# Where the gates times b2 are added in a mixture-of-experts layer: at the 7th, 13th, 19th and 25th expert in place of four experts in a row

## The chip, the cores and the metric

One core of a Trainium2 chip runs the whole kernel. The metric is the device time of one execution in microseconds (us); the kernel before took 1820.64 us, the median of 3 runs (1817.49 to 1822.31).

## The reference

The reference is one layer of a diffusion backbone over 512 latent tokens and 256 context tokens, each of width 1024: a token mixer (an RWKV-7 scan beside a Fourier mix), then a mixture of experts. Only the experts matter here:

```python
logits = h @ w_router + b_router            # h: (512, 1024), 32 experts
top_val, top_idx = lax.top_k(logits, 4)
gates = softmax(top_val)
# for each token t and each of its four experts e:
u   = h[t] @ w1[e] + b1[e]                  # 2048 wide, glu and lin interleaved
act = glu * sigmoid(1.702 * glu) * (lin + 1)   # glu, lin clamped at 7
out[t] += gate[t, e] * (act @ w2[e] + b2[e])
x = layer_norm(alpha * x + gt2 * out)
```

The term `gate * b2` needs no expert's product: over all tokens it is one matrix product, the gates (512 x 32) times b2 (32 x 1024). The kernel computes it in four parts of 128 tokens each. The change is about when these four parts run.

## The kernel before, in words

**The stage.** The expert stage starts at about 700 us of the span and ends at about 1784 us. Experts are sorted by how many tokens chose them; `PLAN` gives the order in which they run and how many rows ("cap") each may have: 128, 32, 160, 32, 96, 64, 96, 192, 32, 64, 96, 64, 160, 32, 96, 64, 96, 192, and so on. In this text e0, e1, ... are the experts in that order, so e7 and e17 are the two of 192 rows. A cap is cut in blocks of 64 rows and a last one of 32 where it isn't a multiple (`blocks`).

**One expert.** `fetch` makes one-hot matrices and indices (TensorE L1249, VectorE L1261 to L1270), casts a selector on GpSimd (L1300, three buffers), and gathers the rows from DRAM by indirect DMAs that GpSimd issues (L1305). `split` transposes them (L1316, L1318). `up` multiplies by w1 in 8 slices, `down` by w2 in 4 slices (L1337); each slice is a tile `raw` of 1 MB that SyncE loads (L1328). `turn` transposes the activations between them (L1389, L1391). `put` adds the rows to `accd` in DRAM by one accumulating indirect DMA per block (L1414), issued by GpSimd; each waits until the one before has landed, as all write the same tensor.

**The ring of weights.** The `raw` tiles have 14 buffers (`RAWA` + `RAWB`). A load is issued as soon as the multiplication that last used its buffer is through; loads run up to 14 slices ahead of TensorE. 384 such loads make the stage's traffic, one after another on SyncE's queue.

**The order.** `all_experts` is a generator of steps, run one by one by `Run`. For its `i`-th expert it yields: the fetch of the expert two ahead, the 8 slices of `up`, then `turn` of the expert before, `split` of the next, the 4 slices of `down` and the `put` of the expert before, and, for four values of `i`, one `b2_part`. Within an engine the final order is that of the planner that builds the program: it simulates the engines and may move a ready instruction ahead of one that it thinks still waits.

**One part of b2.** `b2_part(j)` takes the tile `yb` (128 x 1024, one buffer), and for each half multiplies the gates of 128 tokens by b2 (L1479) into a PSUM tile `pt`, which ScalarE copies into `yb` (L1480). Then GpSimd issues an accumulating indirect DMA of `yb` into `accd` (L1481). The tiles `pt` come from a pool of two buffers that `fetch`, `split` and `turn` use too. b2 was multiplied by gt2 earlier.

Of the kernel before, what the change touches and what calls it, by code (L numbers as in the profile page):

```python
# [1187 lines left out]
def moe(tc, I, ck, h2d, accd, modd, P):  # L1188
# [277 lines left out]
    def place(i):  # L1466
        j, cap = PLAN[i]
        return Expert(cap, rm[:, :, j], R6[:, :, j], sel3[:, j:j + 1])

    def chosen(i):  # L1470
        j = PLAN[i][0]
        return SY.value_load(eidi[0:1, j:j + 1], min_val=0, max_val=NE - 1)

    def b2_part(j):

        y = B.tile([128, D], F32, "yb", 1)
        for n in range(2):
            p = pst.tile([128, 512], F32, name="pt", tag="pt")
            PE.matmul(p, gwT[:, j * 128:(j + 1) * 128], b2r[:, n * 512:(n + 1) * 512], start=True, stop=True)  # L1479
            A.activation(y[:, n * 512:(n + 1) * 512], p, AF.Copy)  # L1480
        G.indirect_dma_start(out=accd[:, :], out_offset=bass.IndirectOffsetOnAxis(ap=toki[:, j:j + 1], axis=0),  # L1481
                             in_=y, in_offset=None, compute_op=ALU.add)

    def all_experts():
        cur, prev = first, None
        ahead = [place(i) for i in range(1, len(PLAN))]
        yield cur.split
        yield ahead[0].fetch
        for i in range(len(PLAN)):
            nxt = ahead[i] if i + 1 < len(PLAN) else None  # L1490
            if i + 2 < len(PLAN):
                yield ahead[i + 1].fetch
            ups = list(cur.up())
            yield from ups[:8 if nxt else 4]
            if nxt:
                nxt.weights(chosen(i + 1))
            if prev:
                yield prev.turn
            if nxt:
                yield nxt.split  # L1500
            if prev:
                yield from prev.down()
                yield prev.put
                if 4 <= i < 8:
                    yield lambda j=i - 4: b2_part(j)
            if not nxt:
                yield from ups[4:]
            prev, cur = cur, nxt
        yield prev.turn
        yield from prev.down()  # L1510
        yield prev.put
# [14 lines left out]
    B = Buffers(None, 99, (praw, RAWA))  # L1526
    first = Expert(PLAN[0][1], rm0, R60, M["sel0"][0:96]).weights(0)
    experts = Run(all_experts())
    experts.load(RAWA)
    sb_ = ExitStack()  # L1530
# [317 lines left out]
```

## Time and profile before

| what | value |
|---|---|
| median of 3 runs | 1820.64 us |
| the profiled execution: its own time | 1815.8 us |
| its span, first to last instruction | 1813.8 us |
| TensorE busy, share of span | 1612.2 us, 89% |
| VectorE, ScalarE, GpSimd busy | 755.1, 392.6, 431.3 us |
| mean DMA rate over the span | 316 GB/s |
| mean granted TensorE clock | 0.929 |

The profiled execution is one run; the numbers of the trace belong to it and not to the median. "Busy" of TensorE is no measure of speed, as its matmuls are pipelined and their ends modelled. In a row of the trace's answers, PE is TensorE, DVE VectorE, ACT ScalarE, POOL GpSimd and SP SyncE; `out<-in` are the program's tile names, and a name in angle brackets behind "idle before" says who ended the wait.

### The profile page before, as it was taken

What the parts mean: (1) busy time and instruction counts of PE and PEld (TensorE: products, weight loads), DVE (VectorE), ACT (ScalarE), POOL (GpSimd) and SP (SyncE); (2) the same over time, 40 slices, a digit from 0 to 9 for tenths busy, and PEclk for the clock granted to TensorE, in tenths of its full rate; (3) what the DMA queues carried; (4) which work ended last, traced back from release to release, by engine and by line L of the source; (5) the groups of instructions that cost most, each with busy time, mean ns of one, the idle gap of its engine ahead of it and who ended that gap; (6) DMA issues with size and microseconds to landing.
All of it is one profiled execution on the core that took longest, in us unless ns stands there. A gap on an engine that the chain in (4) does not pass through costs nothing. (4 is left out here: it accounts for less than half of the span.)

```text
span 1813.8 us, 38967 instructions
## 1 busy us (share of the span) xinstructions
PE 1612.2 (89%) x16148; PEld 875.3 (48%) x16148; DVE 755.1 (42%) x1775; ACT 392.6 (22%) x771; POOL 431.3 (24%) x436
## 2 busy tenths in 40 slices
PE   4889887677999977999959999999999999989982
PEld 1767655566787863454413453443244344324430
DVE  4899977887446674222111121231112211211113
ACT  3565465232223250110010000100000100001002
POOL 1444434264134341101020211111111100112112
PEclk9899888786899977999979999999999999999995
DMA  8567859675575538999996999999899999999995
GB/s 320 168 198 255 252 175 282 182 219 151 174 245 184 201 125 317 414 381 405 416 315 203 386 405 408 412 414 416 340 398 401 411 414 419 408 412 400 402 406 197
DMA packets 205508, 572.72 MB, mean 316 GB/s; under 512 B 28449, under 2 KB 116129, under 8 KB 156177
## 3 DMA queue, kind: packets, MB, share of 16 engines
q1 hardware_dynamic: 144624, 520.11, 73.9%
q0 software_dynamic: 11840, 24.91, 5.9%
q10 hardware_dynamic: 48864, 25.17, 4.8%
q8 instruction: 129, 2.11, 0.5%
q14 instruction: 51, 0.41, 0.1%
HBM read 512.57 MB, written 57.56 MB: 314 GB/s over the span
## 5 line engine op out<-in xcount | busy, mean ns | idle before, releaser
L1337 PE MATMUL st<-raw,xt 128*32 128x512 f32 (+1 forms) x6784 | 634.7, 525 | 18.9 <-DMA raw<-in_w 13.0
L1337 PEld LDWEIGHTS st<-raw,xt 128*32 128x32 f32 x6784 | 244.3, 110 | 368.8 <-issue 285.1
L1337 PE MATMUL st<-raw,at 128*32 128x512 f32 (+1 forms) x3392 | 319.3, 521 | 6.9 <-ACT at L1391 3.1
L1371 DVE TENSOR_SCALAR sg<-st 128x256 f32<-128x256 f32 x87 | 36.4, 419 | 511.5 <-PE st L1344 511.5
L1337 PEld LDWEIGHTS st<-raw,at 128*32 128x32 f32 x3392 | 111.0, 111 | 187.9 <-issue 148.6
L1372 ACT ACTIVATE sth<-sg 128x256 f32<-128x256 f32 x87 | 36.1, 415 | 719.4 <-DVE sg L1371 693.5
L1414 POOL DMA_INDIRECT accd<-y,idx x53 | 86.3, 1628 | 292.6 <-DVE y L1408 145.3
L1408 DVE SCALAR_TENSOR_TENSOR y<-st,gt,gt2h 128x512 f32<-128x512 f32 (+1 forms) x53 | 34.7, 655 | 249.0 <-PE st L1337 215.7
L1305 POOL DMA_INDIRECT xg<-h2d,idx x53 | 53.2, 1004 | 247.7 <-DVE idx L1270 228.4
L1300 POOL CAST sel<-sel 96x64 bf16<-96x64 f32 x31 | 9.2, 298 | 395.3 <-PE st L1344 376.4
L328 PE MATMUL pj<-hhi,wh 128*128 128x512 f32 (+1 forms) x240 | 90.0, 377 | 9.8 <-DVE hlo L281 9.8
L328 PE MATMUL pj<-hhi,wl 128*128 128x512 f32 (+1 forms) x240 | 90.9, 380 | 8.8 <-DVE wl L324 8.8
L328 PE MATMUL pj<-hlo,wh 128*128 128x512 f32 (+1 forms) x240 | 90.9, 379 | 0.0
L652 PE MATMUL big<-Rb,Lt 128*128 128x256 f32 (+1 forms) x192 | 51.9, 420 | 13.4 <-DVE pk L658 5.0
L1391 ACT ACTIVATE at<-pt 128x512 f32<-128x512 f32 (+1 forms) x53 | 26.8, 518 | 143.3 <-PE pt L1389 143.0
L328 PEld LDWEIGHTS pj<-hhi,wl 128*128 128x128 f32 x240 | 47.7, 199 | 20.2 <-DVE wl L324 11.0
L328 PEld LDWEIGHTS pj<-hhi,wh 128*128 128x128 f32 x240 | 47.4, 197 | 19.6 <-DVE hlo L281 10.1
L752 POOL TENSOR_TENSOR SW<-S,Wc 64x128 f32<-64x128 f32 (+1 forms) x66 | 31.3, 475 | 96.4 <-DVE S L787 76.8
L328 PEld LDWEIGHTS pj<-hlo,wh 128*128 128x128 f32 x240 | 47.5, 198 | 13.8 <-issue 7.2
L407 DVE SCALAR_TENSOR_TENSOR acc<-war,sil,acc 128x512 f32<-128x512 f32 x56 | 52.8, 943 | 0.8 <-ACT acc L404 0.6
L1318 ACT ACTIVATE xt<-pt 128x512 f32<-128x512 f32 (+1 forms) x53 | 27.0, 518 | 99.2 <-PE pt L1316 98.7
L652 PEld LDWEIGHTS big<-Rb,Lt 128*128 128x128 f32 x192 | 37.0, 230 | 20.8 <-issue 10.2
(390 smaller groups left out, 2249.3 us busy)
## 6 DMA issues: line engine op xcount, KB each, us to landing
raw<-in_w SPq DMA_DIRECT2D x384, 1024.0 KB
war<-in_w_ada SPq DMA_DIRECT2D x64, 256.0 KB
chd<-pk ACTq DMA_DIRECT2D x52, 256.0 KB
wr<-in_w_in ACTq DMA_DIRECT2D x40, 256.0 KB
wa<-in_w_ada SPq DMA_DIRECT2D x16, 512.0 KB
win<-chd SPq DMA_DIRECT2D x8, 896.0 KB
win<-chd SPq DMA_DIRECT2D x16, 448.0 KB
ltd<-Lt SPq DMA_DIRECT2D x8, 768.0 KB
```

The costliest lines, as they stand in the source:

```text
L328: PE.matmul(p, a[:, k, :], b[:, k0 + k, t0:t0 + n], start=(k0 + k == 0 and i == 0), stop=(k0 + k == KD - 1 and i == 2))
L407: V.scalar_tensor_tensor(acc, wr, sil0[:, k:k + 1], acc, op0=ALU.mult, op1=ALU.add)
L652: PE.matmul(ps[:, z], Lu[:, u0 + (z0 + z if d == 0 else 3 - z0 - z), :], Rb[:, z0 + z], start=True, stop=True)
L752: G.tensor_tensor(SW[HALF[p]].rearrange("p z d c -> p (z d) c"), S[HALF[p], :, :, p].rearrange("p z d c -> p (z d) c"), Wc[HALF[p], 2 * c0 ...
L1305: G.indirect_dma_start(out=x, out_offset=None, in_=h2h[n], in_offset=bass.IndirectOffsetOnAxis(ap=idx[:, 0:1], axis=0))
L1318: A.activation(xt.rearrange("p k s -> p (k s)"), p, AF.Copy)
L1337: PE.matmul(r, x(s * slices + b, o), c(raw[:, b * 2048 // slices:(b + 1) * 2048 // slices]), start=(s + b == 0 and first), stop=(s == n - ...
L1371: V.tensor_scalar(g, u2[:, :, 0], 7.0, None, op0=ALU.min)
L1372: A.activation(t, g, AF.Tanh, scale=0.851)
L1391: A.activation(at.rearrange("p k s -> p (k s)"), p, AF.Copy)
L1408: V.scalar_tensor_tensor(y, st, gt, gt2h[n], op0=ALU.mult, op1=ALU.mult)
L1414: G.indirect_dma_start(out=acch[n], out_offset=bass.IndirectOffsetOnAxis(ap=idx[:, 0:1], axis=0), in_=y, in_offset=None, compute_op=ALU.add)
```

## The change

The condition under which `all_experts` yields a part of b2 is another. Before, the parts came in the turns i = 4, 5, 6 and 7, that is behind the puts of e3, e4, e5 and e6. After, they come in the turns i = 6, 12, 18 and 24, behind the puts of e5, e11, e17 and e23. The part itself is as it was.

```diff
             if prev:
                 yield from prev.down()
                 yield prev.put
-                if 4 <= i < 8:
-                    yield lambda j=i - 4: b2_part(j)
+                if i in (6, 12, 18, 24):
+                    yield lambda j=i // 6 - 1: b2_part(j)
             if not nxt:
                 yield from ups[4:]
```

## Rows read from the trace of the kernel before

**Rows 1.** The page's line of DMA rate, 40 slices of 45.3 us.

```profile
GB/s 320 168 198 255 252 175 282 182 219 151 174 245 184 201 125 317 414 381 405 416 315 203 386 405 408 412 414 416 340 398 401 411 414 419 408 412 400 402 406 197
```

**Rows 2.** Stretches: length, busy us (count) of five engines, clock, DMA share, GB/s.

```profile
920.00:940.00 20.00, 17.53 (x128) 6.65 (x128) 2.08 (x7) 3.06 (x6) 4.23 (x4) 0.89 1.02 396
940.00:960.00 20.00, 13.48 (x120) 3.68 (x123) 1.33 (x6) 1.09 (x2) 5.61 (x4) 0.74 0.72 168
960.00:980.00 20.00, 20.00 (x192) 5.55 (x188) 0.00 (x0) 0.00 (x0) 0.00 (x0) 1.00 0.57 208
980.00:1000.00 20.00, 19.53 (x214) 7.75 (x210) 8.09 (x24) 3.62 (x9) 0.23 (x1) 1.00 0.55 202
1000.00:1020.00 20.00, 19.79 (x260) 10.67 (x256) 5.50 (x18) 3.78 (x7) 5.64 (x5) 1.00 1.02 382
...
1300.00:1320.00 20.00, 16.46 (x164) 5.21 (x158) 7.17 (x24) 2.15 (x5) 6.13 (x4) 0.91 0.72 235
...
1320.00:1760.00 440.00, 423.41 (x4851) 176.19 (x4840) 86.28 (x273) 36.08 (x81) 62.58 (x56) 1.00 1.02 408
```

**Rows 3.** Waits of SyncE's queue, 900 to 1000 us: total us, times, longest.

```profile
SPq L1328 <- PE st L1337: 75.7, 14, 18.7
```

**Rows 4.** Waits of the engines, 760 to 1790 us: total us, times, longest.

```profile
POOL accd L1414 <- DMA accd<-y,idx: 94.9, 18, 9.5
...
ACT yb L1480 <- DMA accd<-yb,toki: 25.6, 2, 17.1
...
PE pt L1249 <- ACT yb L1480: 20.5, 2, 12.0
```

**Rows 5.** Timeline of TensorE (PE): start, length, what, count, idle before.

```profile
884.42 1.98 PE L1479 MATMUL pt<-b2r,gwT 32*128 32x512 f32 x4
...
907.39 0.85 PE L1344 MATMUL st<-b1s,sel 96*32 96x512 bf16 x16
920.24 0.28 PE L1249 MATMUL pt<-R,O 128*32 128x6 bf16 x16 [12.01 <-ACT yb L1480]
...
946.52 0.28 PE L1249 MATMUL pt<-R,O 128*32 128x6 bf16 x16 [8.54 <-ACT yb L1480]
```

**Rows 6.** Timeline of ScalarE (ACT), the copies into yb.

```profile
854.50 0.60 ACT L1480 ACTIVATE yb<-pt 128x512 f32<-128x512 f32 x1 [0.26 <-PE pt L1479]
...
919.59 1.09 ACT L1480 ACTIVATE yb<-pt 128x512 f32<-128x512 f32 x2 [8.51 <-DMA accd<-yb,toki]
...
945.87 1.09 ACT L1480 ACTIVATE yb<-pt 128x512 f32<-128x512 f32 x2 [17.14 <-DMA accd<-yb,toki]
```

**Rows 7.** Timeline of GpSimd (POOL), its queue in order.

```profile
908.39 0.23 POOL L1300 CAST sel<-sel 96x64 bf16<-96x64 f32 x1 [35.26 <-PE st L1344]
909.17 1.58 POOL L1481 DMA_INDIRECT accd<-yb,toki  x1 [0.54 <-ACT sth L1372]
...
939.90 1.57 POOL L1481 DMA_INDIRECT accd<-yb,toki  x1 [6.12 <-issue]
```

**Rows 8.** Stretches of 5 us around the two stops; columns of Rows 2.

```profile
920.00:925.00 5.00, 4.55 (x40) 2.92 (x43) 1.33 (x6) 2.47 (x5) 1.55 (x1) 0.58 1.01 424
...
945.00:950.00 5.00, 3.48 (x32) 0.88 (x35) 1.33 (x6) 1.09 (x2) 2.57 (x2) 0.50 0.34 34
950.00:955.00 5.00, 5.00 (x44) 1.35 (x40) 0.00 (x0) 0.00 (x0) 1.57 (x1) 0.85 0.73 210
```

**Rows 9.** Timeline of SyncE's loads, queried from 909, 951 and 990 us.

```profile
908.74 24.15 SPq L1328 DMA_DIRECT2D raw<-in_w  x5
...
951.86 36.38 SPq L1328 DMA_DIRECT2D raw<-in_w  x8
...
995.46 0.33 SPq L1328 DMA_DIRECT2D raw<-in_w  x1
```

**Rows 10.** Timeline of TensorE in e17, the other expert of 192 rows.

```profile
1273.21 27.70 PE L1337 MATMUL st<-raw,xt 128*32 128x512 f32 x256 [0.61 <-DMA raw<-in_w]
...
1306.10 15.64 PE L1337 MATMUL st<-raw,xt 128*32 128x512 f32 x128 [3.54 <-ACT xt L1318]
```

## The prediction

> **What bounds the kernel now.** I read the page's line of DMA rates first, then cut the stretch where it sags into windows, then asked SyncE's queue what it waited for, and then followed the answer through TensorE, ScalarE and GpSimd.
>
> From slice 16 on the rate stands near 410 GB/s, with one deep sag, 315 and 203 GB/s in the slices from 907 to 997 us, and a small one, 340 GB/s around 1300 us [rows 1]. From 1320 to 1760 us the DMA share is 1.02 at 408 GB/s [rows 2]: the weight loads, 1 MB each, set the pace there, one per 1.049 MB / 408 GB/s = 2.57 us. In the sag the share is 0.72, 0.57 and 0.55 [rows 2]: the loads aren't being issued. What SyncE waits for between 900 and 1000 us is TensorE's products, 75.7 us in 14 waits, the longest 18.7 us [rows 3]. So the ring of 14 buffers is full there and TensorE is late.
>
> TensorE is late because it stood still twice, 12.01 and 8.54 us, both times before a one-hot product (L1249) that wanted a `pt` tile which ScalarE had not yet copied into `yb` [rows 4, 5]. ScalarE in turn waited, 25.6 us in two waits, for the DMA out of `yb` [rows 4, 6]. `yb` has one buffer. Part 0 had filled it at 855.1 us (854.50 + 0.60), but its DMA was issued only at 909.17 us, because GpSimd's queue held a cast ahead of it that waited 35.26 us for TensorE to finish the `up` of e6 [rows 6, 7]. Part 1's products were done at 886.4 us and sat in the two `pt` tiles until 919.6 us; part 2 met the same with part 1's DMA, issued at 939.90 us [rows 5 to 7]. The gain to be had is DMA time lost in the sag, and it is kept to the end, since loads bind again behind it.
>
> **The change part by part.** *How much was lost.* Against 408 GB/s the three windows from 940 to 1000 us moved (168 + 208 + 202) x 20 / 408 = 28.3 us worth of loads in 60 us, a loss of 31.7 us [rows 2]. Counted by DMA share it is 60 - 20 x (0.72 + 0.57 + 0.55) = 23.2 us; I go by the bytes, since the stage is over when they are moved. Both ends are kept: 23 to 32 us.
>
> *What the change takes from TensorE before that loss.* Parts in turns 4 and 5 go from in front of e7: 2 x 1.98 us [rows 5]. Each part now comes six experts behind the last, so `yb` is long empty and both stops go: 12.01 + 8.54 = 20.55 us [rows 5]. The stops had also cost clock: the granted clock was 0.58, 0.50 and 0.85 in the stretches behind them, which at busy times of 4.55, 3.48 and 5.00 us is 1.9 + 1.7 + 0.75 = 4.4 us of work [rows 8]. In sum TensorE reaches its first release in e7 by 4.0 + 20.6 + 4.4 = 28.9 us earlier. The part in turn 6 stays where it was, only as part 0, and the one in turn 7 lies behind e7.
>
> *What is late next.* Not all of the 31.7 us comes back, since e7 has 192 rows and is slower than its loads. Before, its eight slices were given back from 951.86 us on, one in 36.05 / 7 = 5.15 us (36.38 less the last issue's 0.33) [rows 9]. After, the first comes at 951.86 - 28.9 = 922.9 us. The loads queued until then (the last of the five issued in the 24 us from 908.74 us) keep the DMA full until about 940 us, as before [rows 2, 9]. By then four slices of e7 are free (922.9, 928.1, 933.2, 938.4), worth 4 x 2.57 us, to 950.3; the fifth and sixth (943.5, 948.7) carry to 955.4, the seventh (953.8) to 958.0, the eighth comes at 959.0 and ends at 961.5. The next release, the first `down` slice of e6, let its load go at 995.46 us, 7.55 us behind the eighth at 951.86 + 36.05 = 987.91 [rows 9], so now at about 966.5. Idle are 1.0 + 5.0 = 6 us. The gain is 31.7 - 6 = 25.7, say 26 us.
>
> If the planner takes e7 as it took e17, two blocks through all eight slices (27.70 us) and then the third (15.64 us) [rows 10], the slices come free only behind the first pass: from 917.8 + 27.7 + 2 = 947.5 us, and then faster than the loads need them. That idles 7.5 us, with the 3.5 us wait of e17 11 us [rows 10]: a gain of 21 to 24 us. It lies in the forecast's own range.
>
> *What is added at turns 12, 18 and 24.* Three parts of 1.98 us on TensorE, 1.2 us on ScalarE (two copies of 0.60) and 1.58 us on GpSimd [rows 5 to 7]. From 1000 us on the loads bind, and three times 2 us stand far apart, each covered by the ring; without that cover they cost 3 x 1.98 = 5.9 us. They can gain nothing, as they are the same instructions. Bytes and SyncE's queue are unchanged: no load moves past another. On GpSimd each part's DMA waits for the landing of the put before it; such waits were 94.9 us in 18, the longest 9.5 [rows 4]. Behind it queue the cast and the gathers for experts still two ahead, and later puts; the gathers' transposes on TensorE come an expert or more later. I take 0, since the same kind of wait stands between two puts of one expert all through the stage without a sag [rows 2]; the other end is 3 x 9.5 = 28.5 us, if TensorE had to wait out each.
>
> *A rule against it.* The Trainium skill, "Perfetto Trace Analysis", section "Identifying the Most-Contended Engine", says in substance that work should go to the engine or resource in most use. That is the loads here, and by that rule a wait of TensorE is worth nothing: the sum would be 0. The trace agrees for most of the stage (share 1.02) and not for 940 to 1000 us (0.55 to 0.72) [rows 2].
>
> The sum against the profiled execution's own time is 1815.8 - 26 = 1789.8 us (its span of 1813.8 would be about 1788). That execution was 4.8 us under the median of the runs; the median goes from 1820.6 to 1794.6, say 1795 us.
>
> **The rivals.** *More comes back.* The small sag from 1300 to 1320 us (235 GB/s, a loss of (1 - 235 / 408) x 20 = 8.5 us) comes from the order in e17, whose third block was left for a second pass [rows 2, 10]. The planner orders anew, and may take the three blocks together as in e7: 1794.6 - 8.5 = 1786 us. For it: the code of both experts is the same. Against: nothing that the change touches lies in front of e17 but part 1.
>
> *Given back later.* The parts sit in GpSimd's queue before the gathers of coming experts; if in turns 12, 18 and 24 TensorE waits out the landing each time, up to 28.5 us go: 1794.6 + 28.5 = 1823 us, no change. For it: GpSimd's queue was what made part 0 late [rows 7]. Against: gathers run two experts ahead.
>
> *Hidden anyway.* If the loads' average rate were the limit over the whole stage, and the sag only borrowed from the ring, the time would stay at 1820.6 us. Against it speaks that no window behind the sag runs above 408 GB/s to catch up [rows 2].
>
> *Slower.* The planner's new order may put the last block into a second pass at the other experts of three blocks (e2, e7, e12 and e22) too. Each costs what e17 costs, 8.5 us [rows 2, 10]. One or two leave a gain, three are about even with it; with four the time is 1794.6 + 4 x 8.5 = 1829 us. For it: e17 and e7 show that such orders differ by accident. Against: it would have to strike every one, and the sags around those of 160 rows aren't there now [rows 1].
>
> **How the numbers follow.** Chances: forecast 0.72 (own range 1787 to 1805, from 8 us better to 10 us worse than the sum, by the bounds of 23 to 32 us, the 5.9 us uncovered and the two orders of e7); more comes back 0.12; given back 0.07; hidden 0.03; slower 0.06. A change under 0.3%, 5.5 us, can't be told from none. Given back and hidden fall within that: faster 0.84, same 0.10, slower 0.06. The range that leaves out the last three cases and a little of the tails is 1782 to 1809 us.
>
> **What would show it.** ScalarE's wait for the DMA of `yb` and TensorE's wait for ScalarE's copies into `yb` should both be gone from the waits. The clock should stay at 1.00 from 900 to 960 us, the rate from 940 to 1000 us be near 350 GB/s or more in the mean with a short dip of some 6 us, and everything behind 1000 us come 25 to 29 us earlier. The prediction is wrong if TensorE stands before some other tile in e6 or e7 (a gather that is late in GpSimd's queue, say), if a new sag appears near the turns 12, 18 or 24, or if the sag at 940 us stays as deep without the two stops.

## The result, and the profile after

The changed kernel took 1793.83 us, the median of 3 runs (1792.53 to 1795.49), against 1820.64 us before: a ratio of 0.9853, 95% interval 0.9837 to 0.987. In a later session it gave 1797.28 us against 1820.82 us, a ratio of 0.9873 (0.9846 to 0.99). The forecast was 1795 us. The profiled execution took 1793.83 us of its own time, 22.0 us less than the one before (1815.8), where the sum had said 25.7.

The page's rate line of the changed kernel, 40 slices of 44.8 us, answers to [rows 1]:

```profile
GB/s 324 171 195 255 253 184 280 187 209 157 158 242 198 169 150 297 402 375 407 413 412 320 409 414 412 408 413 395 335 413 390 415 411 417 409 404 389 400 407 189
```

The sag of 315 and 203 GB/s is one slice of 320 now; the small one at e17 stands as before, 335 for 340. The same in windows, with the columns of [rows 2] (length, busy us and count of PE, PEld, DVE, ACT and POOL, clock, DMA share, GB/s):

```profile
920.00:940.00 20.00, 20.00 (x192) 7.95 (x188) 0.94 (x4) 0.00 (x0) 2.58 (x2) 1.00 1.02 413
940.00:960.00 20.00, 20.00 (x197) 8.33 (x190) 1.64 (x5) 0.83 (x2) 0.23 (x1) 1.00 0.87 344
960.00:980.00 20.00, 19.53 (x301) 11.97 (x299) 10.25 (x34) 2.79 (x7) 6.89 (x5) 1.00 0.86 280
980.00:1000.00 20.00, 19.79 (x178) 7.12 (x178) 1.60 (x4) 2.58 (x5) 0.54 (x2) 1.00 1.02 409
1260.00:1280.00 20.00, 20.00 (x204) 6.15 (x200) 1.93 (x8) 0.60 (x1) 4.16 (x3) 1.00 0.94 345
1280.00:1300.00 20.00, 19.53 (x190) 6.24 (x182) 4.71 (x15) 2.79 (x7) 4.38 (x4) 1.00 0.86 304
1300.00:1740.00 440.00, 424.56 (x4824) 180.35 (x4816) 87.42 (x276) 36.62 (x82) 63.07 (x56) 1.00 1.02 405
```

At 408 GB/s the two windows from 940 to 980 us lose (1 - 344/408) x 20 + (1 - 280/408) x 20 = 9.4 us, where 31.7 were lost [rows 2]. The granted clock, 0.89 and 0.74 in the two windows from 920 to 960 us before, is 1.00 throughout. SyncE's waits between 900 and 1000 us, and every wait of 760 to 1790 us that names `yb` (total us, times, longest), answer to [rows 3, 4]:

```profile
SPq L1328 <- PE st L1337: 48.8, 18, 7.0
```

```profile
ACT yb L1480 <- PE pt L1479: 30.7, 8, 18.6
POOL accd L1414 <- DMA accd<-yb,toki: 10.7, 2, 9.6
```

SyncE's longest wait fell from 18.7 to 7.0 us. ScalarE's wait for the DMA of `yb` (25.6 us) and TensorE's for ScalarE's copies (20.5 us) have no row any more. What ScalarE waits for now is the product itself; no row of these waits has an engine that waits for ScalarE's copies. TensorE's timeline through the turn of part 0 and e7 has no idle time of note, in answer to [rows 5]:

```profile
913.89 1.98 PE L1479 MATMUL pt<-b2r,gwT 32*128 32x512 f32 x4
915.79 3.20 PE L1337 MATMUL st<-raw,xt 128*32 128x512 f32 x26
...
919.36 38.31 PE L1337 MATMUL st<-raw,xt 128*32 128x512 f32 x352
```

### The profile page after: what moved, and what is told of

Same layout as the page of the kernel before. It is cut to its first block, busy times and chain, and to the rows that moved or that the text cites. A ratio compares the mean times of both kernels' runs of the same rounds, so it can differ in the third digit from the quotient of the medians.

```text
span 1791.8 us, 38976 instructions
## 1 busy us (share of the span) xinstructions
PE 1609.1 (90%) x16148; PEld 885.5 (49%) x16148; DVE 755.7 (42%) x1775; ACT 391.5 (22%) x771; POOL 429.3 (24%) x436
## 5 line engine op out<-in xcount | busy, mean ns | idle before, releaser
L1337 PEld LDWEIGHTS st<-raw,xt 128*32 128x32 f32 x6784 | 254.3, 110 | 355.3 <-issue 278.3
L328 PEld LDWEIGHTS pj<-hhi,wl 128*128 128x128 f32 x240 | 47.1, 196 | 20.1 <-DVE wl L324 10.7
```

What stands on the lines that cost most here:

```text
L328: PE.matmul(p, a[:, k, :], b[:, k0 + k, t0:t0 + n], start=(k0 + k == 0 and i == 0), stop=(k0 + k == KD - 1 and i == 2))
L1337: PE.matmul(r, x(s * slices + b, o), c(raw[:, b * 2048 // slices:(b + 1) * 2048 // slices]), start=(s + b == 0 and first), stop=(s == n - ...
```

## The experiments

One measure serves all of them: the **loss** is the sum of (1 - rate / 408) x 20 us over the 20 us windows between 740 and 1740 us that moved less than 385 GB/s. The kernel before loses 44.1 us, the changed one 21.7 us in its first profile and 18.7 us in a second. The difference of the first two, 22.4 us, is that of the two profiled times (22.0): both issue their first load at 622 us and take 53 us behind the last. The other windows average 406.8 to 408.6 GB/s in every kernel here, so the loss holds most of what differs within the stage. A ratio in the table is to runs of the kernel before from the same session, whose medians were 1819.66 to 1822.12 us. The edits of e7, e1 and e2 are shown against the kernel before, the others against the changed one.

| kernel | median us | ratio to before (95%) | loss us | windows under 385 GB/s (start: GB/s) |
|---|---|---|---|---|
| before | 1820.64 | 1 | 44.1 | 780: 354, 940: 168, 960: 208, 980: 202, 1000: 382, 1300: 235 |
| changed | 1793.83 | 0.9853 (0.9837-0.987) | 21.7 | 780: 353, 940: 344, 960: 280, 1260: 345, 1280: 304, 1620: 380 |
| changed, again (a_after) | 1797.28 | 0.9873 (0.9846-0.99) | 18.7 | 780: 366, 960: 237, 1280: 267, 1620: 381 |
| two buffers for yb (e1) | 1816.43 | 0.9963 (0.9949-0.9978) | 31.6 | 800: 361, 920: 379, 960: 212, 980: 381, 1000: 382, 1120: 271, 1460: 226 |
| no b2 (e2) | 1790.93 | 0.9828 (0.9806-0.9851) | 18.6 | 780: 368, 960: 296, 1260: 281, 1280: 307 |
| four in a row, late (e3) | 1817.29 | 0.9986 (0.9962-1.0009) | 43.8 | 780: 353, 940: 384, 960: 311, 1260: 195, 1560: 139, 1580: 357, 1600: 383, 1620: 366, 1640: 290 |
| one pair in a row (e5) | 1808.07 | 0.9916 (0.9895-0.9937) | 27.1 | 780: 359, 960: 151, 980: 381, 1280: 189 |
| no DMA of yb (e7) | 1790.72 | 0.9831 (0.9803-0.9858) | 20.3 | 780: 374, 940: 375, 960: 180, 980: 383, 1280: 354, 1440: 367 |

For the changed kernel run again I had expected a ratio of 0.983 to 0.987 and a loss near 22 us; it came out at 0.9873 and 18.7 us, so the loss of one kernel differs by some 3 us between executions, far less than the 22 us gained.

**The DMA of yb left out (e7).** The sharpest cut: products and copies stay in turns 4 to 7, and what makes the copies wait goes. With it go 2 MB of accumulation, and the planner writes the order anew.

```diff
             A.activation(y[:, n * 512:(n + 1) * 512], p, AF.Copy)
-        G.indirect_dma_start(out=accd[:, :], out_offset=...(ap=toki[:, j:j + 1], axis=0),
-                             in_=y, in_offset=None, compute_op=ALU.add)
```

> The kernel before with its four parts in turns 4 to 7, but without their accumulating DMAs: products and copies into the one yb are made, the result lacks gate times b2. Theory (only the wait of the copies for those DMAs stopped TensorE): no stop, the loads lose 9 to 14 us between 940 and 1010 us in place of 31.7; 1787 to 1800 us, the lower end if the 2 MB of accumulation are worth something besides. Rival (the products and copies in front of e7 cost by themselves): 1808 to 1820 us.

Measured: 1790.72 us and a loss of 20.3 us. No wait for a DMA of `yb` is left; of the waits of 760 to 1790 us one row names `yb`:

```profile
ACT yb L1480 <- PE pt L1479: 25.6, 8, 8.6
```

So the products and copies in front of e7 are not what cost; the wait for the DMAs was. Around e7 the windows at 940, 960 and 980 us lose 1.6 + 11.2 + 1.2 = 14 us, the upper end of what was expected, where 33.0 were lost before. Not all of the 30 us by which the time fell are the stops': 19.0 us are, 5.9 us come from a smaller dip at e17 (2.6 for 8.5 us), and the accumulations that are missing are worth an estimated 8 us of load time (see the run without b2).

**Two buffers (e1).**

```diff
-        y = B.tile([128, D], F32, "yb", 1)
+        y = B.tile([128, D], F32, "yb", 2)
```

> The kernel before, its four parts still in turns 4 to 7, with two buffers for yb in place of one. Theory (the wait for the one buffer stops TensorE, and that stops the loads): TensorE's waits for ScalarE's copies into yb (20.5 us before) fall to under 2 us, the loads lose about 10 to 14 us between 940 and 1000 us in place of 31.7, since e7 starts some 4 us later than in the changed kernel (two parts of 1.98 us more in front of it); time 1794 to 1802 us. Rival (four accumulating DMAs close together in GpSimd's queue and on the DMA engines are what costs): they are as close as before, so the time stays at 1812 to 1822 us.

The mechanism came out and the time did not: 1816.43 us. TensorE's wait for the copies is gone, and the loss at e7 (windows from 920 to 1020 us) is 1.4 + 9.6 + 1.3 + 1.3 = 13.6 us where 31.7 and 1.3 were lost before. But the planner wrote another order, and two new dips came, windows of this kernel at e12 and e22:

```profile
960.00:980.00 20.00, 19.53 (x200) 8.35 (x196) 8.09 (x24) 3.62 (x9) 2.35 (x3) 1.00 0.71 212
...
1120.00:1140.00 20.00, 16.97 (x240) 8.81 (x232) 8.36 (x30) 1.94 (x5) 4.16 (x4) 0.91 0.72 271
1280.00:1300.00 20.00, 20.00 (x204) 6.12 (x200) 1.33 (x6) 0.60 (x1) 0.99 (x1) 1.00 1.01 422
1460.00:1480.00 20.00, 16.45 (x236) 8.32 (x232) 9.72 (x33) 3.11 (x8) 6.63 (x5) 0.91 0.61 226
```

The timeline of TensorE in its e12 shows why. The expert of 160 rows is taken in two passes, as e17 was before [rows 10]: two blocks through all eight slices, then the last block, after a wait for its transposed rows.

```profile
1097.37 27.65 PE L1337 MATMUL st<-raw,xt 128*32 128x512 f32 x256
...
1129.48 2.63 PE L1337 MATMUL st<-raw,xt 128*32 128x256 f32 x27 [3.03 <-ACT xt L1318]
```

No slice comes free in the first pass, and the loads stop: 6.7 us lost at e12 and 8.9 us at e22, while e17 lost its 8.5 us dip (422 GB/s at 1280 us). From the last load's issue to the end of the span it also took 1816.0 - 1752.9 = 63.1 us, against 1813.8 - 1760.4 = 53.4 us before. At the end of GpSimd's queue in this kernel the last accumulations wait for each other behind the last load:

```profile
1776.26 1.55 POOL L1414 DMA_INDIRECT accd<-y,idx  x1 [6.80 <-DMA accd<-y,idx]
1780.93 1.55 POOL L1414 DMA_INDIRECT accd<-y,idx  x1 [3.11 <-issue]
1785.94 1.55 POOL L1414 DMA_INDIRECT accd<-y,idx  x1 [3.46 <-DMA accd<-y,idx]
```

So 12.5 us less are lost in the stage and 9.7 us of that go again behind it; 2.8 us are left, where the medians of the session differ by 5.7 us. The "slower" rival of the prediction, a second pass at other experts, is real: it struck two here.

**All four left out (e2).**

```diff
-                if 4 <= i < 8:
-                    yield lambda j=i - 4: b2_part(j)
```

> The four parts are left out altogether, so the result lacks gate times b2. Theory (the parts in turns 12, 18 and 24 cost nothing, the one in turn 6 costs TensorE 2 us in front of e7): 1789 to 1795 us, the loads' loss at e7 2 us smaller than the 9.4 us of the changed kernel. Rival (each part still costs where it stands, by GpSimd's queue or by its 0.5 MB of accumulation): 3 x 2 to 3 x 9.5 us less, 1765 to 1788 us.

1790.93 us, in the theory's range: the ratio is 0.9828 against 0.9853 and 0.9873 of the changed kernel, with intervals that overlap. The loss at e7 is 5.5 us, 3.9 us under the 9.4 of the changed kernel's first profile and 2.9 under the 8.4 of its second, where 2 us had been forecast.

That the parts in turns 12, 18 and 24 cost nothing does not follow, though. From the 89th issue of a load to the last the changed kernel took 832.3 and 830.1 us in its two profiles (906.2 to 1738.5 and 911.1 to 1741.2), 813.4 and 813.5 without its losses from 900 us on. The kernel before took 854.2 us, without losses 812.7; this one 821.2 and 804.5; e7 823.0 and 804.4. So the four accumulations are worth an estimated 8 to 9 us of load time, some 2 us each, as much in the old places as in the new. e1, e3 and e5, which hold them too, stand at 809.7, 808.4 and 814.4, so this is good to a few us. Here it does not show in the time because this execution issued its first load 6.5 us later than the changed kernel's (628.9 for 622.4 us) and took 57.5 us behind the last load, for 53.3.

**One pair in a row (e5).**

```diff
-                if i in (6, 12, 18, 24):
-                    yield lambda j=i // 6 - 1: b2_part(j)
+                if i in (5, 6, 18, 24):
+                    yield lambda j=(5, 6, 18, 24).index(i): b2_part(j)
```

> Parts in turns 5, 6, 18 and 24: one pair in a row, just ahead of e7. Theory (each stop costs about its length there): one stop of 8 to 13 us and some clock behind it, the loads lose 18 to 26 us around e7; 1802 to 1811 us. Rival (the gain came from the planner's new order in general and not from the stops): no stop matters, 1790 to 1797 us.

1808.07 us, in the theory's range, but not by the path that it named. TensorE stopped once, and behind e7's `up`, not ahead of it, and for 6.04 us. And ScalarE did not wait for a DMA of `yb` there: its two copies stood behind activations of e7, which waited for that `up`. Rows of TensorE, then of ScalarE:

```profile
962.34 1.48 PE L1344 MATMUL st<-b1s,sel 96*32 96x512 bf16 x24
969.86 0.28 PE L1249 MATMUL pt<-R,O 128*32 128x6 bf16 x16 [6.04 <-ACT yb L1480]
...
963.24 0.42 ACT L1372 ACTIVATE sth<-sg 128x256 f32<-128x256 f32 x1 [47.68 <-DVE sg L1371]
...
969.23 1.07 ACT L1480 ACTIVATE yb<-pt 128x512 f32<-128x512 f32 x2
```

The window from 960 us falls to 151 GB/s, and the loss at e7 is 12.6 + 1.3 = 13.9 us for 9.4 in the changed kernel. Of the 14 us by which the median is above the changed kernel's that is 4.5 us, about a third. The rest is a deeper dip at e17 (10.7 for 8.2 us), a longer end (59.2 us behind the last load, for 53.3) and a later start of the loads (626.9 for 622.4 us). A pair brought a stop back, but by ScalarE's order and not by the DMA; whether the planner put the copies there because of the one buffer stays open.

**Four in a row, late (e3).**

```diff
-                if i in (6, 12, 18, 24):
-                    yield lambda j=i // 6 - 1: b2_part(j)
+                if 23 <= i < 27:
+                    yield lambda j=i - 23: b2_part(j)
```

> The four parts in a row again, with one buffer, but in turns 23 to 26, where the ring holds only 8 to 12 slices ahead of TensorE and not 13. Theory (a stop of TensorE costs only when the ring is full): ScalarE waits for yb again, 10 us or more in total, TensorE stops for 5 to 20 us, but the loads lose under 6 us there; 1792 to 1802 us. Rival (a stop costs its own length wherever it comes): 1805 to 1816 us.

Neither theory's number came out: 1817.29 us. I had expected a stop of 5 to 20 us. It was one of 38.68 us, because part 0's DMA stood behind four accumulations, besides casts and gathers, in GpSimd's queue, from 1470 us, when part 0 was in `yb`, to 1559 us. Rows of this kernel from TensorE's, ScalarE's and GpSimd's timelines:

```profile
1569.21 0.28 PE L1249 MATMUL pt<-R,O 128*32 128x6 bf16 x16 [38.68 <-ACT yb L1480]
...
1568.56 1.08 ACT L1480 ACTIVATE yb<-pt 128x512 f32<-128x512 f32 x2 [36.67 <-DMA accd<-yb,toki]
...
1549.91 1.55 POOL L1414 DMA_INDIRECT accd<-y,idx  x1 [7.76 <-DMA accd<-y,idx]
1559.09 1.55 POOL L1481 DMA_INDIRECT accd<-yb,toki  x1 [7.63 <-issue]
```

What the ring does is seen in the windows of the stop:

```profile
1540.00:1560.00 20.00, 0.00 (x0) 0.00 (x0) 0.00 (x0) 0.00 (x0) 4.03 (x3) 0.50 1.03 403
1560.00:1580.00 20.00, 10.10 (x100) 4.17 (x102) 2.65 (x12) 2.94 (x6) 5.75 (x5) 0.61 0.57 139
1580.00:1600.00 20.00, 20.00 (x242) 8.78 (x239) 2.02 (x7) 1.20 (x2) 4.20 (x3) 1.00 0.99 357
```

TensorE does nothing for 20 us and the loads run on at 403 GB/s; then the ring is full, and the two windows behind lose 13.2 + 2.5 = 15.7 us. The three from 1600 to 1660 us lose 1.2 + 2.1 + 5.8 = 9.1 us more, where the changed kernel loses 1.4; how much of that comes from the stop is not shown. So the stop cost the loads some 16 to 23 of its 38.7 us and not its own length: the ring, not full at that point, took the rest. That much of the theory stands, and the rival of equal length is refuted, though the time came out just above that rival's range. The single buffer and GpSimd's queue made the trouble at this place too.

**Other places for the big experts (e4, e6).** The losses left are at e7 and e17, both of 192 rows. In two kernels I moved them to turns 12 and 22.

```diff
-    for j, rest in zip((3, 1, 4, 2, 5, 6), ((32, 96, 64, 96), ...
+    for j, rest in zip((3, 4, 1, 5, 2, 6), ((32, 96, 64, 96), ...      # e4
+    for j, rest in zip((3, 6, 1, 4, 2, 5), ((32, 96, 64, 96), ...      # e6
```

> The changed kernel with another order of the big experts: the two of 192 rows come as the 13th and 23rd (turns 12 and 22) in place of the 8th and 18th, and ones of 160 rows take their places. Theory (the 9.4 and 8.2 us that the loads still lose at e7 and e17 come from 192 rows being slower than their loads while the ring is full): in turns 12 and 22 the ring holds some 10 slices and not 13, so the losses shrink, from 21.7 us in all to 8 to 14 us; 1780 to 1788 us. Rival (the loss follows the 192 rows or the planner's order wherever they stand): 1790 to 1797 us.

> As the run before it, with the big experts in the order 160, 128, 192, 160, 192, 160 rows. Theory: the first place with a full ring now has the lightest of them, so TensorE catches up there, and the losses stay at 8 to 14 us in all; 1780 to 1788 us. Rival: the last one, of 160 rows, now stands near the end and takes back what was won; 1788 to 1797 us.

e4 took 1797.52 us (ratio 0.9867, 0.9838 to 0.9895), no different from the changed kernel beside it at 0.9873; its loss is 19.0 us. e6 took 1804.34 us (0.9904) with a loss of 29.4 us, outside the ranges of both theory and rival. My theory fell. The dip at e7 does go in both (1.6 us are left in e4, none in e6), but others come; the windows of e4 at its e7, e12 and e22:

```profile
960.00:980.00 20.00, 19.53 (x256) 10.52 (x252) 9.16 (x27) 3.23 (x8) 1.82 (x2) 1.00 0.97 376
1100.00:1120.00 20.00, 18.12 (x185) 5.59 (x180) 4.66 (x16) 1.92 (x4) 5.17 (x4) 1.00 0.84 327
1120.00:1140.00 20.00, 19.43 (x196) 6.40 (x194) 5.77 (x21) 2.43 (x6) 4.23 (x3) 1.00 0.87 303
1440.00:1460.00 20.00, 19.51 (x220) 6.46 (x216) 7.80 (x28) 2.16 (x5) 0.00 (x0) 1.00 0.92 349
```

The loss follows the planner's order and not the 192 rows alone, which was the other half of the rival. In these dips no load is issued for 16 to 29 us, and then several close together: some of an expert's blocks were left for a second pass, and only that pass gives its slices back. SyncE's queue of e4, queried from 1098 and 1439 us, and of e6 from 1600 us; the issues before these stand at 1096.8, 1437.5 and 1598.1 us:

```profile
1122.59 17.43 SPq L1328 DMA_DIRECT2D raw<-in_w  x9
...
1456.15 17.79 SPq L1328 DMA_DIRECT2D raw<-in_w  x10
...
1626.71 32.71 SPq L1328 DMA_DIRECT2D raw<-in_w  x16
```

In e4 these are the two of 192 rows, which lose 9.1 and 2.9 us. In e6 one such dip is at e12 of 192 rows (8.9 us, with a wait of TensorE of 4.40 us for a gather), but others are at e24 of 96 rows (5.8 us, no load from 1503.0 to 1518.7 us) and at e27 of 160 (8.2 us), while the second expert of 192 rows, e22, loses nothing (407 GB/s from 1460 to 1480 us).

**A shorter and a longer ring (e8_ring12, e8_ring15).**

```diff
-RAWA, RAWB = 4, 10
+RAWA, RAWB = 4, 8       # 12 buffers
+RAWA, RAWB = 4, 11      # 15; act64 7 buffers, at64 4
```

> The changed kernel with 12 buffers for weight slices in place of 14. Theory (loads are lost where TensorE is slower than they for longer than the ring covers, 2.57 us per buffer): two buffers fewer cost some 5 us at each of e7 and e17 and as much at one or two other big experts, so the losses rise from about 20 to 30 or 40 us; 1804 to 1816 us. Rival (the ring's depth is no matter, the losses at e7 and e17 come from the products alone): 1793 to 1799 us.

> The changed kernel with 15 buffers for weight slices; to make room the activations of 64 rows have 7 buffers (8 before) and their transposes 4 (5 before). Theory: 2.57 us less lost at each of e7, e17 and e2; 1786 to 1793 us by that alone. Rival (the planner's new order decides more than one buffer): anything from 1787 to 1805 us, with the losses in other places.

With 12 buffers the time was 1816.72 us (0.998, 0.9965 to 0.9995) and the loss 34.2 us, both about as the theory had them, the time just past its upper end. The places are not the theory's: e7 lost 3.1 us, less than with 14 buffers, and e17 18.4 us (354, 114 and 380 GB/s from 1260 to 1320 us), so a price per buffer is not shown. With 15 it was 1811.03 us (0.9946, 0.9928 to 0.9965) and the loss 27.8 us: more than with 14, with 13.3 us of it at e17 (208 and 336 GB/s at 1280 and 1300 us) and new dips at 1160 and 1180 us. One buffer more did not pay. As fewer buffers for `act64` and `at64` came with it, whether these or the planner's order undid it stays open.

## Why the prediction was right

**The stops.** Right, and shown: both waits are gone from the changed kernel, and e7, which takes the DMAs away and leaves the parts in a row, wins back 19 of the 33.0 us lost there. The first load that waited for a slice of e7 was issued at 922.42 us, against the 922.9 that 28.9 us of earlier work had given. Before it stood at 951.86 [rows 9]. This is its row in SyncE's timeline, queried from 922 us:

```profile
922.42 0.33 SPq L1328 DMA_DIRECT2D raw<-in_w  x1
```

**What e7 keeps.** This is the term that was mis-sized: 9.4 us (8.4 in the second profile) and not 6, which makes the sum 31.7 - 9.4 = 22.3 us in place of 25.7. In windows of 5 us:

```profile
950.00:955.00 5.00, 5.00 (x53) 1.95 (x48) 0.00 (x0) 0.00 (x0) 0.00 (x0) 1.00 0.85 315
955.00:960.00 5.00, 5.00 (x57) 2.37 (x50) 1.64 (x5) 0.83 (x2) 0.23 (x1) 1.00 0.62 216
960.00:965.00 5.00, 4.53 (x45) 1.62 (x47) 5.00 (x16) 2.79 (x7) 1.68 (x1) 1.00 0.87 239
965.00:970.00 5.00, 5.00 (x72) 2.68 (x66) 1.44 (x5) 0.00 (x0) 1.91 (x1) 1.00 0.57 213
970.00:975.00 5.00, 5.00 (x107) 3.36 (x103) 2.60 (x10) 0.00 (x0) 0.85 (x1) 1.00 0.97 279
```

I had the DMA dry for 1 us at 958 and for 5 us up to 966.5. It fell from 951 on and came back only at 975. The releases were not what was wrong: the last load that waited for a slice of e7 was issued at 958.14 us and the next, for the first `down` slice of e6, at 965.69, against 959.0 and 966.5 in the sum. Three things were left out. Between 915 and 950 us the loads ran at 418 GB/s in the mean, so the waiting slices were used up about 1 us sooner. A load that has the DMA to itself does not fill it: the shares are 0.85 and 0.62 in the windows from 950 and 955 us, where the sum had the queue at full rate to 958, and 0.57 in the one from 965 us, which begins with the wait for it. And part 0's own DMA, which the sum had not counted there, left GpSimd's queue in the dip, at 965.98 us: from 970 to 975 us the DMA share is 0.97, but the rate 279 GB/s.

```profile
965.98 1.91 POOL L1481 DMA_INDIRECT accd<-yb,toki  x1 [4.08 <-issue]
```

How the 3.4 us divide among the three is not shown. An idle stretch counted by whole slices leaves out its ramp on either side.

**The added parts.** Taken as 0, and shown as 0 to within 1 us for the move: without the losses the loads took 812.7 us before and 813.4 and 813.5 after. The accumulations cost an estimated 2 us each of load time, but in either place. A dip of 1.4 us at 1620 us stands beside the DMA of part 3, issued at 1618.0 us, in the first profile, and one of 1.3 us in the second. No gather stopped TensorE in e6 or e7; at e17 two waits for one, of 1.37 and 1.21 us, stand in its timeline.

**The clock.** It was 1.00, the higher of its two levels (2.4 GHz), from 900 to 1000 us, as forecast; the 4.4 us put on it agree with the load at 922.42 us, though no run took it by itself.

**The rivals.** *Hidden anyway*, and with it the Trainium skill's "Perfetto Trace Analysis", section "Identifying the Most-Contended Engine", read over the whole stage, is refuted: TensorE's waits were worth 22 us, though over most of the stage the loads were the resource in most use. Read for 940 to 1000 us alone, where the DMA share was 0.55 to 0.72 [rows 2], the rule does not say that. The argument that the prediction gave against this rival was misread: slices and windows behind the sag do run above 408 GB/s (419 in [rows 1]), so their rate refutes nothing; the result does. *More comes back* did not happen: e17 lost 8.2 us, for 8.5. Its last block again came in a second pass, only without the stop of 3.54 us [rows 10]: after an issue at 1258.03 us SyncE's queue has none until this row, queried from 1262 us.

```profile
1282.19 13.21 SPq L1328 DMA_DIRECT2D raw<-in_w  x8
```

*Given back later* and *slower* did not happen in this kernel, but second passes took 15.6 us in e1, and e4 and e6 had them too. The chance of 0.06 for *slower* was perhaps low; that the order around the big experts stayed good here was partly luck.

**The medians.** The profile's 22.0 us and the medians' 26.8 us differ because the profiled execution before was 4.8 us under its median; the second session's ratio of 0.9873 is 23 us. Everything behind 1000 us came 22 us earlier (the last load at 1738.5 for 1760.4 us), not the 25 to 29 that the prediction gave as a sign. That the median came so close to 1795 us owes something to that difference, which is luck.

## What to carry to other kernels

Where loads bind a stage on average, look for the windows where they don't: a wait of another engine costs there what the buffers ahead no longer cover, not its own length. A tile with one buffer that leaves by a queue shared with waiting instructions is free only when that queue gets to it; measure that time before spacing its uses: from filling to issue it was 54 us for part 0 in the kernel before and 89 us in e3. And when an edit makes a planner write the order anew, judge the mechanism by its own waits and windows: in e1 the waits went as meant, and the new order took 15.6 us at two other places.

## What the runs showed of the hardware that was not expected

The first load of the stage was issued at 622.3 and 622.4 us in the first profiles of before and after, at 627.6 us in the changed kernel's second, and between 621.1 (e3) and 633.1 us (e4) in the others. What stands ahead of the stage thus varies by 5 us between executions of one kernel and by 12 us over all of them, and the span carries it to the end. Spans of single profiles are therefore best compared from a common point, such as the 89th load.

Accumulating 0.5 MB into DRAM by one indirect DMA cost the loads an estimated 2 us, while the DMA engines counted as busy: 380 GB/s at a share of 1.03 in the window from 1620 us, where part 3 of the changed kernel was added beside gathers and puts of rows, against 405 GB/s at 1.02 from 1300 to 1740 us.
